# The first norm of a hybrid decoder: squares summed by two other routes, and new prices in the planner

## The chip, the cores and the metric

The kernel runs on one core of a Trainium2 chip. A core has five engines that work side by side, each through its own list of instructions in order: TensorE (PE; its weight loads are shown as PEld), VectorE (DVE), ScalarE (ACT), GpSimd (POOL) and SyncE (SP), which issues the DMA transfers. They wait for each other by semaphores. The metric is the time of one execution on the device in microseconds (us), lower is better. All times here are of executions on the chip.

## What is computed

Two layers over 1024 tokens of width 1024, in float32: a gated DeltaNet layer, then a layer with stick-breaking attention, each with a SwiGLU feed-forward and a gated per-layer embedding. The change concerns the first norm of the first layer:

```python
def rms_norm(x, g):
    xf = x.astype(jnp.float32)
    y = xf * lax.rsqrt(jnp.mean(xf * xf, axis=-1, keepdims=True) + EPS)
    return (y * g.astype(jnp.float32)).astype(x.dtype)

h = x
for i in range(DEPTH):
    hn = rms_norm(h, ln_mix[i])
    ...  # mixer, feed-forward, per-layer embedding
```

## The kernel before

Activations lie with features on the 128 partitions and tokens along the row: x is eight tiles (k = 0 to 7) of 128 features by 1024 tokens, and is worked on in two halves of 512 tokens (hf = 0, 1). Matrix products run on TensorE with float32 split in two parts, hi and lo, each rounded to float32r: a product is three passes (hi by hi, hi by lo, lo by hi), each with 512 columns. A unit is 128 output features of one half: 8 k times 3 passes, 24 products. Weights come by DMA into `raw` (two buffers); ScalarE casts them to `whi`, and VectorE or GpSimd subtracts to get `wlo`.

**What sets the order.** The program is written as Python generators: small tasks (a norm, the features of one head, a copy of a result) that issue a few instructions and yield. The class `Flow` steps through them at build time and keeps a clock for each engine with a price for each instruction (`cost`), a delay from one engine to the next (`lat`, `LAT`) and the time of transfers (`issued`). The task that is ready and has the best priority issues next, and where none is ready the stream of large products (`fill`) goes on. The engines' lists are thus fixed before the run. A price that changes can reorder instructions anywhere behind it; no instruction becomes longer or shorter by it.

**The start.** `gdn_start` holds four tasks. `load` issues the sixteen loads of x (`xT`, 256 KB each) on SP, in tiles named kt, Z, vt, QK, zz and ou. `norm(hf)` squares each of the eight tiles of a half on ScalarE (`sumsq`; scratch tiles Gb, four buffers), and VectorE adds the squares up in `LT`. Then `rstd` lets TensorE sum over the partitions: the sum tile is the stationary operand, a column of ones the moving one, so there are four products with one column each, one per 128 tokens, into a tile `tp`. `root` makes `ms` on VectorE and raises it to the power -1/2 on GpSimd (`rs`). `normed` broadcasts `rs` over the partitions with four products into another `tp`, and for each k VectorE multiplies x by it and the gain (`qf<-..,vec,tp`), ScalarE casts the result to float32r (`x<-qf`), and VectorE subtracts for the lo part (`x<-qf,x`).

Meanwhile `warm` issues products `mm<-triR` with 256 columns, whose results nobody reads, until the planner holds the first normed tile to be ready. Then `gdn_first` issues the first units of both halves, k by k as the tiles come: `ab` (tile `po`), k and q of head 0 (tiles `mm`, two buffers). For each unit `gdn_features` then empties `mm` on ScalarE (`xe<-mm`) and runs a short convolution over it (`ca`). `loads` issues the weights; it starts once all loads of the first half of x are issued.

**Behind the start** come the units of the first heads. `gdn_inv` prepares the decay matrices: broadcast loads `Gb<-gD`, a selection on GpSimd and 16 exponentials on ScalarE (`Gb<-Gb,nG`). `ple_products` makes the products of the second layer's embedding (tiles `rc`, `r`, `po`, `mm`); ScalarE copies each result to `sg` or `ca`, two buffers each, from which SP writes it to DRAM (`ppD`).

In the profile nearly every instruction has line 64, the helper through which all are issued, so tiles tell them apart.

Of the kernel before, what the change touches and what calls it, by code (L numbers as in the profile page):

```python
# [10 lines left out]
AF = mybir.ActivationFunctionType  # L11
ALU = mybir.AluOpType
# [3 lines left out]
P = 128  # L16
S = 1024
D = 1024
NK = D // P
H = 8  # L20
HW = 512
# [61 lines left out]
class Flow:  # L83
# [30 lines left out]
    def cost(self, eng, op, out, ins, kw):  # L114
        n = 1
        for d in (ins[0] if op == "tensor_reduce" else out).shape[1:]:
            n *= d
        psum = any(x.space == PSUM for x in ins)
        if eng == "pe":
            if op != "transpose" and ins[0].dtype == F32R:  # L120
                return max(n, P) / 2400.0 + 0.0127
            return max(n, P) * (2 if op == "transpose" else 4) / 2400.0 + (0.003 if op == "transpose" else 0.0107)
        if eng == "dve":
            if op == "memset":
                return 0.06 + n / 3840.0
            tail = 0.06 if any(x.shape[-1] == 1 for x in ins) and n > 1 else 0.0
            if any(x.shape[-1] > 1 and x.ap[-1][0] > 1 for x in ins):
                tail += 0.085
            fast = op in ("tensor_copy", "tensor_scalar") and not psum
            return 0.069 + tail + n / (1920.0 if fast else 960.0)  # L130
        if eng == "act":
            us = (0.052 if psum else 0.094) + n / 1200.0
            return us + 0.093 * (len(ins) - 1) + (0.235 if "accum_out" in kw else 0.0)
        if op == "tensor_tensor":
            return 0.295 + 0.166 * n if kw.get("op") == ALU.pow else 0.148 + n * 0.002104
        return 0.4 + n / 1400.0 if op == "affine_select" else 0.1 + n / 1085.0

    def shared(self, eng, op, outs, ins, kw, t, c):

# [22 lines left out]
    def issued(self, eng, op, args, kw):  # L162
        aps = [x for x in list(args) + list(kw.values()) if hasattr(x, "space")]
        if not aps:
            if op == "preload_act_table_set":
                self.table = 3
            return
        outs = [kw["out"] if "out" in kw else aps[0]]
        if "accum_out" in kw:
            outs.append(kw["accum_out"])  # L170
        ins = [x for x in aps if not any(x is o for o in outs)]
        t = self.clock[eng]
        if eng == "pe":
            t = max(t, self.now)
        spans = []
        for x, w in [(o, True) for o in outs] + [(i, False) for i in ins]:
            if x.space == DRAM:
                lo, dims = x.offset, x.ap
            else:
                dims, step = x.ap[1:], x.ap[0][0]  # L180
                lo = x.offset % step if step else x.offset
            hi = lo + 1 + sum((c - 1) * d for d, c in dims)
            rec = self.mem.get(x.name)
            if rec is None:
                rec = self.mem[x.name] = {}
                old = self.old.pop(x.name, None)
                if old is not None and old in self.mem:
                    t = max([t] + [max(v[0] + self.lat(v[1], eng), v[2] + self.lat(v[3], eng)) for v in self.mem.pop(old).values()])
            for (l, h), v in rec.items():
                if l < hi and lo < h:  # L190
                    if not (w and eng == v[1]):
                        t = max(t, v[0] + self.lat(v[1], eng))
                    if (w or x.space == PSUM) and v[3] != eng:
                        t = max(t, v[2] + self.lat(v[3], eng))
            spans.append((rec, (lo, hi), w))
        if eng == "dma":
            n = 4
            for d in outs[0].shape:
                n *= d
            run = min(x.ap[-1][1] if x.ap[-1][0] == 1 else 1 for x in outs + ins)  # L200
            n *= max(1, P // run)
            self.clock["dma"] = t + 0.475
            self.rings = max(self.rings, t + 1.1) + n / 360e3
            end = self.rings
        else:
            c = self.cost(eng, op, outs[0], ins, kw)
            f = [x for x in args if isinstance(x, AF)]
            if f and f[0] in TABLES and TABLES[f[0]] != self.table:
                self.table = TABLES[f[0]]
                t += 1.4  # L210
            if eng in ("dve", "pool"):
                t = self.shared(eng, op, outs, ins, kw, t, c)
            end = t + c
            self.clock[eng] = end
            if eng == "pe":
                self.now = end
        for rec, key, w in spans:
            v = rec.setdefault(key, [-1e9, eng, -1e9, eng])
            if w:
                v[0], v[1] = end, eng  # L220
            elif end > v[2]:
                v[2], v[3] = end, eng
        self.ready = max(self.ready, end + self.LAT[eng])

    def lat(self, a, b):
        if b == "pe":
            return {"pe": 0.0, "dma": 1.2}.get(a, 0.25)
        return 0.13 if a == b and a != "dma" else self.LAT[a]

    def run(self, fill):  # L230
        test = None
# [40 lines left out]
class Net:  # L272
# [155 lines left out]
    def weights(self):  # L428

        flow, nc = self.flow, self.nc  # L430
        reqs = self.weight_list()
# [10 lines left out]
                return "e"  # L442

        def loads():
            yield lambda: ("x", 0, NK - 1) in flow.at
            for key, src, _, _ in reqs:
                yield lambda: count["load"] - count["split"] < 2
                raw = self.t(self.wp, "raw", (P, NK, P), bufs=2)
                nc.sync.dma_start(raw, src)
                raws.append((raw, flow.ready))  # L450
                count["load"] += 1
                yield 0.5
# [39 lines left out]
        def splits():  # L492
            for i, (key, src, gain, cls) in enumerate(reqs):
# [12 lines left out]
                flow.spawn(done(), 3)  # L506

        flow.spawn(loads(), 4)
        flow.spawn(splits(), 3)

# [30 lines left out]
    def root(self, pool, st, r):  # L541
        nc = self.nc
        ms = self.t(pool, "ms", (P, 4))
        nc.vector.tensor_scalar(ms, st[:, :4], 1.0 / D, EPS, op0=ALU.mult, op1=ALU.add)
        self.unbank(st)
        yield
        nc.gpsimd.tensor_tensor(r, ms, self.nhalf[:, :4], op=ALU.pow)
        yield
# [136 lines left out]
    def gdn_start(self):  # L685

        nc, io, flow = self.nc, self.io, self.flow
        tags = ["kt"] * 4 + ["Z"] * 3 + ["vt"] * 3 + ["QK"] * 2 + ["zz"] * 2 + ["ou"] * 2
        src = {(hf, k): self.g(tags[hf * NK + k]) for hf in range(2) for k in range(NK)}

        def load():
            for hf in range(2):
                for k in range(NK):
                    nc.sync.dma_start(src[hf, k], io["xT"][k, :, hf * HW : (hf + 1) * HW])
                    flow.mark(("x", hf, k))
                    yield 0.4
            nc.sync.dma_start(self.ad, io["ad"])
            nc.sync.dma_start(self.conv, io["conv"])
            nc.sync.dma_start(self.masks, io["cst"][:, C_OFF:])
            nc.vector.memset(self.X0, 0.0)  # L700

        def norm(hf):
            acc = self.g("LT", (P, 2, HW))[:, 0]
            for k in range(NK):
                yield lambda: flow.done(("x", hf, k))
                yield from self.sumsq(lambda: self.g("Gb"), acc, src[hf, k], k == 0)
            r = self.g("rs", (P, 4))
            yield from self.rstd(self.gs, acc, r)
            yield from self.normed(("n0", hf), r, lambda k: src[hf, k], self.vec[:, 0], lambda: self.g("qf"))

        def ple():
            yield lambda: flow.done(("norm", ("n0", 1)))
            self.ple1 = [[self.g(tag, dt=F32R) for tag in tags] for tags in (("Z", "Z", "Z", "QK"), ("ou", "ou", "zz", "zz"))]
            flow.mark("ple1")
            yield from self.ple_operands(1, *self.ple1, "kt")

        flow.spawn(load(), 0)
        flow.spawn(norm(0), 0)
        flow.spawn(norm(1), 1)
        flow.spawn(ple(), 4)  # L720

# [1347 lines left out]
def layout(inputs):  # L2069

    g = {k: np.asarray(v) for k, v in inputs.items()}
# [12 lines left out]

    a = {}
    a["cst"] = const_table()
    a["xT"] = np.ascontiguousarray(g["x"][0].T).reshape(NK, P, S)
    a["pT"] = np.ascontiguousarray(g["p"][:, 0].transpose(0, 2, 1)).reshape(2, 2, P, S)
    vs = []
# [40 lines left out]
```

## Time and profile before

| | us |
|---|---|
| median of 3 runs | 2787.19 |
| lowest, highest run | 2784.03, 2788.08 |
| the profiled execution | 2787.44 |
| its span, first to last instruction | 2785.7 |

A row of the timeline has start and duration in us, the engine, the operation, output<-inputs by the program's names, shapes and a count of merged instructions; in brackets stands how long the engine had been idle before it, and for whom it waited. A row of a group has the count, the busy time in us and the mean of one in ns, then the idle time before them. A row of a window has its length, then busy time and number of instructions for each engine, TensorE's granted clock as a share of full speed, the busy share of the DMA engines and GB/s. TensorE's products overlap, and their ends are modelled: how far apart they start tells more than how long each one lasts. A product of plain float32 is recorded as two instructions.

### The profile page before, as it was taken

To read this page: it belongs to the slowest core of one execution; us is meant where nothing else is said; L and a number is where in the kernel's file an instruction comes from. 1 tells how busy PE (TensorE), PEld (TensorE's weight loads), DVE (VectorE), ACT (ScalarE), POOL (GpSimd) and SP (SyncE) were. 2 spreads that over 40 slices of the span, in tenths; PEclk is the share of its full clock that TensorE was granted. 3 is DMA by queue.
4 is the path that set the end of the run, shared out by engine and by line. 5 is a ranking of instruction groups with operands and counts; after the bars stand their busy time and mean duration, and the time that the engine had idled before them with its cause. 6 is when DMAs were issued, how large, how long until landed. Compare 5 with 4: busy or idle time off the path is not lost.

```text
span 2785.7 us, 37779 instructions
## 1 busy us (share of the span) xinstructions
PE 2741.7 (98%) x13203; PEld 2278.1 (82%) x13203; DVE 1951.7 (70%) x3733; ACT 1324.3 (48%) x2701; POOL 860.4 (31%) x742
## 2 busy tenths in 40 slices
PE   9999999999999999999999999999999999999999
PEld 8788888888778888888778888888878888888777
DVE  7687887873875665477857778887686565557783
ACT  6655555543433344322335778877443343322241
POOL 0111111100166667444101222221036666643400
PEclk9999999999999999999999999999999999999999
DMA  4412222247334444587232111114514444487623
GB/s 147 143 58 76 75 82 74 74 151 244 140 110 159 155 155 144 223 328 304 106 131 99 54 50 61 54 58 158 200 57 156 150 148 151 144 311 284 262 90 105
DMA packets 165072, 394.85 MB, mean 142 GB/s; under 512 B 34000, under 2 KB 35344, under 8 KB 155408
## 3 DMA queue, kind: packets, MB, share of 16 engines
q1 hardware_dynamic: 164880, 392.43, 39.5%
q8 instruction: 104, 1.70, 0.2%
q14 instruction: 88, 0.72, 0.1%
HBM read 273.77 MB, written 118.59 MB: 141 GB/s over the span
## 4 chain that ended last, share of the span: by engine, by line
PE 86%; DVE 7%; ACT 4%; issue 2%; DMA 1%; POOL 1%; ACTq 0%; POOLq 0%
PE dn L64 38%; PE mm L64 34%; PE tp L64 4%; PE z L64 3%; PE c L64 2%; PE o L64 2%; DVE x L64 1%; PE po L64 1%; PE rc L64 1%; PE r L64 1%; DVE u L64 1%; ACT junk L64 1%; ACT L64 1%; DVE v L64 1%; PE st L64 1%
## 5 line engine op out<-in xcount | busy, mean ns | idle before, releaser
L64 PE MATMUL mm<-x,whi 128*128 128x512 f32 x2848 | 939.0, 400 | 8.7 <-DVE x L64 5.4
L64 PEld LDWEIGHTS mm<-x,whi 128*128 128x128 f32 x2848 | 528.5, 189 | 106.7 <-DVE x L64 7.9
L64 PE MATMUL mm<-x,wlo 128*128 128x512 f32 x1424 | 568.5, 399 | 0.0
L64 PE MATMUL dn<-x,whi 128*128 128x512 f32 x1776 | 548.7, 390 | 1.8 <-DVE x L64 0.9
L64 POOL TENSOR_TENSOR wlo<-raw,whi 128x512 fp32r<-128x512 f32 x236 | 345.5, 1485 | 442.7 <-ACT whi L64 413.2
L64 ACT CAST whi<-raw 128x1024 fp32r<-128x1024 f32 x231 | 242.8, 1051 | 447.4 <-DVE raw L64 244.7
L64 PEld LDWEIGHTS dn<-x,whi 128*128 128x128 f32 x1776 | 333.3, 188 | 73.3 <-DVE x L64 2.6
L64 PE MATMUL dn<-x,wlo 128*128 128x512 f32 x888 | 345.7, 389 | 0.0
L64 PEld LDWEIGHTS mm<-x,wlo 128*128 128x128 f32 x1424 | 269.0, 189 | 46.4 <-issue 0.3
L64 PE MATMUL dn<-hx,whi 128*128 128x512 f32 x864 | 267.4, 390 | 0.4 <-DVE hx L64 0.2
L64 DVE TENSOR_TENSOR tt<-u,tt 128x512 fp32r<-128x512 f32 x140 | 143.9, 1028 | 81.5 <-ACT tt L64 81.5
L64 PEld LDWEIGHTS dn<-x,wlo 128*128 128x128 f32 x888 | 166.7, 188 | 34.4
L64 PEld LDWEIGHTS dn<-hx,whi 128*128 128x128 f32 x864 | 162.8, 189 | 35.0 <-DVE hx L64 0.6
L64 DVE TENSOR_TENSOR v<-v,dn 128x512 f32<-128x512 f32 x112 | 76.5, 684 | 155.4 <-PE dn L64 155.0
L64 DVE TENSOR_TENSOR wlo<-raw,whi 128x512 fp32r<-128x512 f32 x226 | 153.9, 693 | 27.2 <-ACT whi L64 26.9
L64 PE MATMUL dn<-hx,wlo 128*128 128x512 f32 x432 | 169.1, 391 | 3.4 <-POOL wlo L64 3.4
L64 POOL TENSOR_TENSOR wlo<-sw,whi 128x512 fp32r<-128x512 f32 x102 | 144.3, 1431 | 2.0 <-ACT whi L64 2.0
L64 ACT CAST tt<-u 128x512 fp32r<-128x512 f32 x140 | 84.8, 619 | 123.5 <-DMA yD<-tt 100.2
L64 DVE TENSOR_TENSOR E<-E,dn 128x512 f32<-128x512 f32 x132 | 90.0, 684 | 71.4 <-PE dn L64 69.1
L64 POOL TENSOR_TENSOR rs<-ms,nhalf 128x4 f32<-128x4 f32 x11 | 12.3, 1122 | 330.7 <-DVE ms L64 330.7
L64 PE MATMUL dn<-y,whi 128*128 128x512 f32 x352 | 108.4, 389 | 0.0
L64 DVE SCALAR_TENSOR_TENSOR ca<-xe,conv,ca 128x512 f32<-128x512 f32 x144 | 106.2, 744 | 0.9 <-ACT ca L64 0.4
(376 smaller groups left out, 5124.8 us busy)
## 6 DMA issues: line engine op xcount, KB each, us to landing
yD<-tt SPq DMA_DIRECT2D x296, 256.0 KB, 2.4
x<-yD SPq DMA_DIRECT2D x58, 1024.0 KB, 11.3
raw<-f_s SPq DMA_DIRECT2D x84, 512.0 KB, 3.7
raw<-d_s SPq DMA_DIRECT2D x40, 512.0 KB, 5.9
raw<-w_in SPq DMA_DIRECT2D x33, 512.0 KB, 4.0
hx<-yD SPq DMA_DIRECT2D x16, 1024.0 KB, 14.5
x<-oD SPq DMA_DIRECT2D x26, 512.0 KB, 5.8
raw<-g_out SPq DMA_DIRECT2D x16, 512.0 KB, 5.2
```

Source lines behind the costliest of these rows:

```text
L64: r = issue(*args, **kw)
```

## The change

It has two parts.

**The first norm.** For the first half TensorE sums the squares itself: each of the eight square tiles is the stationary operand of four one-column products that accumulate in one `tp` tile, with no adds on VectorE. For the second half a copy of x with tokens on the partitions, `xr` (4 blocks of 128 tokens by 1024 features, 512 KB each, made on the host from the same input), is loaded into `LT` tiles, and ScalarE squares each with `accum_out`, which leaves the sums in `ms` without TensorE. The four loads of `xr` come ahead of the second half of `xT`; `LT` has two buffers, so the third and fourth wait for squares of the first two. The first two weights are issued ahead of `xr` (the mark `first`); that weights start after the eighth x tile is as before (`NK` is 8). The zeroing of `X0` moves from VectorE to GpSimd, to the very start.

**The prices.** Short float32r products have a floor of 0.1 us; a subtraction on GpSimd costs a little more and a selection less; a load that spreads one row over all partitions lands 1.4 us later; and two instructions of VectorE in a row need 0.06 us between them in place of 0.13.

```diff
@@ cost, issued, lat
-                return max(n, P) / 2400.0 + 0.0127
+                return max(n / 2400.0 + 0.0127, 0.1)
...
-            return 0.295 + 0.166 * n if kw.get("op") == ALU.pow else 0.148 + n * 0.002104
-        return 0.4 + n / 1400.0 if op == "affine_select" else 0.1 + n / 1085.0
+            return 0.295 + 0.166 * n if kw.get("op") == ALU.pow else 0.169 + n * 0.002125
+        return 0.119 + n / 960.0 if op == "affine_select" else 0.1 + n / 1085.0
...
+            spread = any(x.ap[0][0] == 0 for x in ins)
-            self.rings = max(self.rings, t + 1.1) + n / 360e3
+            self.rings = max(self.rings, t + (2.5 if spread else 1.1)) + n / 360e3
...
-        return 0.13 if a == b and a != "dma" else self.LAT[a]
+        return {"dve": 0.06, "dma": self.LAT["dma"]}.get(a, 0.13) if a == b else self.LAT[a]
@@ loads (weights)
-            yield lambda: ("x", 0, NK - 1) in flow.at
-            for key, src, _, _ in reqs:
+            yield lambda: ("x", 0, 7) in flow.at
+            for n, (key, src, _, _) in enumerate(reqs):
+                if n == 2:
+                    flow.mark("first")
@@ gdn_start: load
+        rows = {}
             for hf in range(2):
+                if hf == 1:
+                    yield lambda: "first" in flow.at
+                    for j in range(4):
+                        rows[j] = self.g("LT", (P, 2, HW))
+                        nc.sync.dma_start(rows[j].rearrange("p a c -> p (a c)"), io["xr"][j])
+                        flow.mark(("xr", j))
+                        if j == 1:
+                            yield lambda: flow.done("sq1")
+                        else:
+                            yield 0.4
...
-            nc.vector.memset(self.X0, 0.0)
@@ gdn_start: norm
-            acc = self.g("LT", (P, 2, HW))[:, 0]
-            for k in range(NK):
+            r = self.g("rs", (P, 4))
+            if hf == 0:
+                st = yield from self.bank()
+            else:
+                ms = self.t(self.gs, "ms", (P, 4))
+                for j in range(4):
+                    yield lambda: flow.done(("xr", j))
+                    nc.scalar.activation(rows[j], rows[j], AF.Square, accum_out=ms[:, j : j + 1])
+                    if j == 1:
+                        flow.mark("sq1")
+                yield
+                yield from self.root(self.gs, ms, r)
+            for k in range(NK * (1 - hf)):
                 yield lambda: flow.done(("x", hf, k))
-                yield from self.sumsq(lambda: self.g("Gb"), acc, src[hf, k], k == 0)
-            r = self.g("rs", (P, 4))
-            yield from self.rstd(self.gs, acc, r)
+                sq = self.g("Gb")
+                nc.scalar.activation(sq, src[hf, k], AF.Square)
+                yield
+                for j in range(4):
+                    self.mmul(st[:, j : j + 1], sq[:, j * P : (j + 1) * P], self.ones[:, :1], k + j == 0, k == NK - 1, True)
+            if hf == 0:
+                yield
+                yield from self.root(self.gs, st, r)
...
+        nc.gpsimd.memset(self.X0, 0.0)
@@ layout (host)
+    a["xr"] = np.ascontiguousarray(g["x"].reshape(S, D)[HW:].reshape(4, P, D))
```

How the lists move is shown at three places. The first is TensorE's list from its start (`x4`, `x73` and the like count equal instructions in a row; `ones` is a part of `cst`). Before:

```order
L64 MATMUL mm_126<-triR 128x256 x73
L64 MATMUL tp_32_252<-cst,LT_128 128x1 x4
L64 MATMUL mm_126<-triR 128x256 x16
L64 MATMUL tp_38_286<-cst,rs_251 128x128 x4
L64 MATMUL mm_126<-triR 128x256 x36
L64 MATMUL po_351<-x_291,whi_246 128x512 x2
```

There the fillers in front, between and behind the sum and the broadcast are 125. TensorE's list from its start, after the change:

```order
L64 MATMUL mm_127<-triR 128x256 x22
L64 MATMUL tp_19_131<-cst,Gb_154 128x1 x4
L64 MATMUL tp_19_131<-cst,Gb_167 128x1 x4
L64 MATMUL tp_19_131<-cst,Gb_174 128x1 x4
L64 MATMUL tp_19_131<-cst,Gb_180 128x1 x4
L64 MATMUL tp_19_131<-cst,Gb_186 128x1 x4
L64 MATMUL tp_19_131<-cst,Gb_192 128x1 x4
L64 MATMUL tp_19_131<-cst,Gb_198 128x1 x4
L64 MATMUL tp_19_131<-cst,Gb_204 128x1 x4
L64 MATMUL mm_127<-triR 128x256 x14
L64 MATMUL tp_40_247<-cst,rs_130 128x128 x4
L64 MATMUL mm_127<-triR 128x256 x21
```

The fillers are 57 now, and eight groups of one-column products stand in a row with none between them.

The second place is SP's list behind the first eight loads of x. After the change (before, the loads of `xT` go on to ou there, with two loads of `raw` between them):

```order
L64 DMA raw_210<-w_in 128x1024
L64 DMA raw_225<-w_in 128x1024
L64 DMA LT_236<-xr 128x1024
L64 DMA raw_238<-w_in 128x1024
L64 DMA LT_245<-xr 128x1024
L64 DMA raw_257<-w_in 128x1024
L64 DMA LT_313<-xr 128x1024
L64 DMA LT_319<-xr 128x1024
L64 DMA vt_118<-xT 128x512
```

Four weights and the four blocks of `xr` now stand ahead of the second half of `xT`, of which vt_118 is the first.

The third place is ScalarE's list around the first exponentials of `Gb`. Before (688, 777, 829 and 883 are units that follow the first q on TensorE, in this order):

```order
L64 COPY xe_774<-mm_688 128x512
L64 ACT_TABLE_LOAD
L64 ACTIVATE EE<-vt_690 128x192
L64 ACT_TABLE_LOAD
L64 ACTIVATE beta<-vt_635 128x64
L64 COPY xe_824<-mm_777 128x512
L64 CAST whi_826<-raw_714 128x1024
L64 ACTIVATE ca_833<-xe_774,conv 128x512
L64 ACTIVATE ca_837<-xe_824,conv 128x512
L64 ACT_TABLE_LOAD
L64 ACTIVATE Gb_724<-Gb_724,nG 128x128 x4
```

The units 688 and 777 are copied out of `mm` ahead of the exponentials. ScalarE's list at the same place after the change, where the units behind the first q are 636, 713, 791 and 830:

```order
L64 COPY xe_710<-mm_636 128x512
L64 ACTIVATE EE<-vt_619 128x192
L64 ACT_TABLE_LOAD
L64 ACTIVATE beta<-vt_579 128x64
L64 ACT_TABLE_LOAD
L64 ACTIVATE qf_747<-ca_683 128x512
L64 ACTIVATE ca_753<-xe_710,conv 128x512
L64 ACT_TABLE_LOAD
L64 ACTIVATE Gb_650<-Gb_650,nG 128x128 x4
L64 ACTIVATE Gb_651<-Gb_651,nG 128x128 x4
L64 ACTIVATE Gb_658<-Gb_658,nG 128x128 x4
L64 ACTIVATE Gb_659<-Gb_659,nG 128x128 x4
```

The copy of unit 713 is no longer ahead of the exponentials: it is the next instruction behind these rows, and unit 830 uses the same buffer of `mm` as 713.

More of the change, by code (lines that the diff above doesn't have):

```diff
@@ L544, in root @@
         nc.vector.tensor_scalar(ms, st[:, :4], 1.0 / D, EPS, op0=ALU.mult, op1=ALU.add)
-        self.unbank(st)
+        if st.name in self.held:
+            self.unbank(st)
         yield
```

## The prediction

> **What bounds the kernel now.** The page's head comes first, to see which engine sets the end: busy time, share of the span and instructions of each.
>
> ```profile
> span 2785.7 us, 37779 instructions
> PE 2741.7 (98%) x13203; PEld 2278.1 (82%) x13203; DVE 1951.7 (70%) x3733; ACT 1324.3 (48%) x2701; POOL 860.4 (31%) x742
> ```
>
> TensorE is idle for 2785.7 - 2741.7 = 44.0 us in all. So a change to the first norm can win only what TensorE does not spend on real products: idle time, fillers, and time at a low clock. The timeline of the start, rows of several engines in order, shows the fillers (`mm<-triR`, results thrown away).
>
> ```profile
> 4.20 11.50 PE L64 MATMUL mm<-triR 128*128 128x256 f32 x73 [4.20 <-DVE triR L64]
> 7.64 0.63 ACT L64 ACTIVATE LT<-kt 128x512 f32<-128x512 f32 x1 [5.56 <-DMA kt<-xT]
> 15.54 0.95 PE L64 MATMUL tp<-cst,LT 128*128 128x1 f32 x8
> 16.77 1.38 POOL L64 TENSOR_TENSOR rs<-ms,nhalf 128x4 f32<-128x4 f32 x1 [16.26 <-DVE ms L64]
> 18.34 1.05 PE L64 MATMUL tp<-cst,rs 128*128 128x128 f32 x8
> 19.15 4.56 PE L64 MATMUL mm<-triR 128*128 128x256 f32 x36
> 21.96 0.68 DVE L64 TENSOR_TENSOR x<-qf,x 128x512 fp32r<-128x512 f32 x1
> 23.55 0.62 PE L64 MATMUL po<-x,whi 128*128 128x512 f32 x2
> 43.27 0.62 PE L64 MATMUL po<-x,whi 128*128 128x512 f32 x2
> ```
>
> Sums of squares are ready for the root at 16.49, the first real product starts at 23.55, and the products of the second half start at 43.27. The product at 23.55 is held by the 36 fillers: its operand was complete at 22.64. From there on it is busy throughout, as this window behind it shows (length, then the busy time of TensorE, its weight loads, VectorE, ScalarE, POOL):
>
> ```profile
> 54.35:79.99 25.64, 25.64 (x124) 20.75 (x123) 16.59 (x38) 25.22 (x47) 4.26 (x6) 1.00 0.32 106
> ```
>
> So 43.27 is the mark against which I measure the start.
>
> **The squares on TensorE.** The change drops the seven adds on VectorE for each half (14 in all) and gives TensorE eight groups of four products with one column each, recorded as eight instructions.
>
> ```profile
> L64 DVE TENSOR_TENSOR LT<-LT,Gb 128x512 f32<-128x512 f32 x14 | 9.5, 681 | 5.3 <-ACT Gb L64 4.8
> 4.00:9.00 5.00, 4.80 (x22) 4.80 (x23) 0.22 (x2) 1.34 (x3) 0.00 (x0) 1.00 0.87 279
> 9.00:14.00 5.00, 5.00 (x41) 5.00 (x40) 4.31 (x7) 4.18 (x7) 0.00 (x0) 1.00 1.04 405
> ```
>
> An add took 0.68 us against 0.63 us for its square, so the adds kept pace with ScalarE and only the last one stood on the path. A group of one-column products took 0.95 us (row of 15.54). Fillers cost 4.80/22 = 0.218 us each in the first window and 5.00/41 = 0.122 us in the second: TensorE starts at half its rate, although the clock column reads 1.00 there. Now 22 fillers come first: 4.20 + 22 x 0.218 = 9.0. Eight groups at 0.95 us end at 16.6, against 16.49 before. **Even at full clock the squares are ready no earlier.**
>
> But will the clock be full? Here are windows further on; behind the busy times stands the granted clock.
>
> ```profile
> 2692.00:2696.00 4.00, 2.58 (x16) 1.78 (x14) 4.00 (x7) 0.96 (x2) 0.00 (x0) 1.00 0.47 154
> 2696.00:2699.00 3.00, 3.00 (x11) 2.40 (x10) 2.28 (x5) 0.89 (x2) 1.01 (x1) 0.53 0.37 147
> 2040.00:2044.00 4.00, 4.00 (x15) 3.52 (x14) 0.51 (x1) 0.00 (x0) 3.53 (x3) 0.50 0.39 131
> 98.00:104.00 6.00, 2.48 (x13) 1.77 (x11) 3.27 (x9) 2.22 (x10) 1.01 (x1) 1.00 0.68 214
> 2037.05 1.51 PE L64 MATMUL st<-cst,acc 128*128 128x1 f32 x8 [0.28 <-DVE acc L64]
> 2038.41 0.77 PE L64 MATMUL mm<-hx,whi 128*128 128x512 f32 x1
> ```
>
> After a stretch with idle time and one group of one-column products (2692 to 2696) the clock was halved, and it stayed halved through 2040 to 2044 although TensorE was busy. One-column products therefore seem to count as little work. At half clock such a group takes 2038.41 - 2037.05 = 1.36 us. Eight of them in a row are a far longer such stretch, so I expect the half clock: 9.0 + 8 x 1.36 = 19.9, or about 18.3 if the first groups still run at full clock.
>
> [...]
>
> **To the first product.** VectorE's ms, then POOL's root (1.38), need about 1.7 us, and 14 fillers lie over that: 1.7 us at 0.122, 3.0 at half clock (0.218). The broadcast of the root is 1.05 us (1.5 in the ratio 1.36 to 0.95), then 21 fillers 2.6 us. Full clock: 16.6 + 1.7 + 1.05 + 2.6 = 21.95. Half, until the fillers have released it: 19.9 + 3.0 + 1.05 + 2.5 = 26.4 (24.4 from the other start). Before: 23.55.
>
> The first half is then 72 products, paced by these:
>
> ```profile
> 23.16 0.74 DVE L64 SCALAR_TENSOR_TENSOR qf<-kt,vec,tp 128x512 f32<-128x512 f32 x1
> 23.82 0.68 DVE L64 TENSOR_TENSOR x<-qf,x 128x512 fp32r<-128x512 f32 x1
> 54.15 0.61 PE L64 MATMUL mm<-x,whi 128*128 128x512 f32 x2
> L64 ACT CAST x<-qf 128x512 fp32r<-128x512 f32 x13 | 8.0, 619 | 12.8 <-DVE qf L64 12.8
> L64 ACT ACTIVATION_READ_ACCUMULATOR junk<-tp 128x1 f32 x8 | 1.6, 196 | 0.0
> ```
>
> The 48 products from 43.27 to 54.15 took 0.227 us each, so 72 take 16.3, and the second broadcast 1.05. For six products (1.36 us) VectorE makes one multiply (0.66 to the next start) and one subtraction (0.68 at most): without the adds, and with the zeroing of X gone to POOL (where nothing waits for it: POOL idles until 16.77), it just keeps up, save for two splits of weights. ScalarE's squares of 1024 columns with a sum have no row: they lie between twice a square's 0.63 and that plus a read of the accumulator, 0.2; I take 1.3, as it is nearer the second. Four make 5.2 us, and eight casts 5.0, which hides under 17 us. If rows of x came late, the casts queued behind the square on ScalarE would wait, and through them VectorE and the products. I count 1.5 us of such waits at full clock and 0.5 at half, where all else is earlier than needed. Marks: 21.95 + 17.4 + 1.5 = 40.8 (**-2.5**), or 26.4 + 17.4 + 0.5 = 44.3 (+1.0), or 42.3 to 43.0 from 24.4 (-0.6). I take **+0.4** for the half clock, between the two and nearer the first: the 22 fillers alone end before or about when the fast window of 9 to 14 begins. SP now sends x's second half last, behind a square (LT has two buffers) and behind splits; some 2.9 MB at the 400 GB/s of the window are in by 36 to 38, before use. If that cover went, each us late would cost a us.
>
> **ScalarE after the start.** These are groups of ScalarE between 54.3 and 80 (busy, mean ns, idle), and the rows at the ends.
>
> ```profile
> L64 ACT ACT_TABLE_LOAD x8 | 10.3, 1283 | 0.1
> L64 ACT CAST whi<-raw 128x1024 fp32r<-128x1024 f32 x4 | 4.2, 1041 | 0.0
> L64 ACT ACTIVATE ca<-xe,conv 128x512 f32<-128x512 f32 x4 | 2.8, 717 | 0.0
> L64 ACT COPY xe<-mm 128x512 f32<-128x512 f32 x4 | 2.3, 576 | 1.0 <-PE mm L64 1.0
> 54.35 0.59 ACT L64 COPY xe<-mm 128x512 f32<-128x512 f32 x1 [0.98 <-PE mm L64]
> 79.99 4.79 ACT L64 ACTIVATE Gb<-Gb,nG 128x128 f32<-128x128 f32 x16
> 85.99 0.40 PE L64 MATMUL rc<-Z,whi 128*128 128x512 f32 x1
> ```
>
> ScalarE has no slack here: the 16 exponentials start 25.64 us after the copy at 54.35. Now one table load, one cast, one copy and one ca fewer stand ahead of them (1.28 + 1.04 + 0.58 + 0.72 = 3.6 us busy, 3.4 as each starts a little before the last has ended), so they start 22.25 us after it and end 4.8 later. But the copy that empties `mm` for the last unit of v (24 products) now stands **behind** them: 22.25 + 4.8 + 0.5 and 0.4 for signals = 27.9 us after the end of the first units. TensorE gets there after 85.99 - 54.15 = 31.84, less that unit's 5.44 and 0.81 for eight transpositions (18.34 to 19.15 is such a group): 25.6. So it waits **2.3 us** where it did not wait before. Bounds: 0 if ScalarE gains on the rows, 4 if the clock halves in the gap.
>
> **The first products of the embedding**, with their waits:
>
> ```profile
> 92.36 1.16 PE L64 MATMUL tp<-qf,kf 128*128 128x128 f32 x8 [0.47 <-ACT vt L64]
> 103.72 0.50 PE L64 MATMUL r<-Z,whi 128*128 128x512 f32 x1 [3.52 <-ACT sg L64]
> 112.24 0.50 PE L64 MATMUL mm<-Z,whi 128*128 128x512 f32 x1 [1.78 <-ACT ca L64]
> 103.08 0.59 ACT L64 COPY sg<-r 128x512 f32<-128x512 f32 x1 [3.08 <-DMA ppD<-sg]
> 98.70 0.39 SPq L64 DMA_DIRECT2D ppD<-sg  x1
> ```
>
> The 3.52 us are a chain: SP holds the write of sg until 98.70 behind a second load of eGb, so ScalarE gets its buffer back at 103.08. After the change the copies alternate between ca and sg, but the first write stands behind the same load, and a copy that waits for it stands ahead of a kf that TensorE needs: about 4.3 us there against 3.52 + 1.78 + 0.47 = 5.77. I take **-1.5**, bounds -5.8 and +2.
>
> **The rest.** The planner's prices also reorder the delta rule and the attention; the feed-forward keeps TensorE's order. Such waits are small already:
>
> ```profile
> 1934.27 0.50 PE L64 MATMUL o<-wh,vh 128*128 128x512 f32 x1 [1.05 <-DVE wh L64]
> 1935.00:1942.00 7.00, 6.62 (x20) 5.63 (x21) 4.24 (x12) 4.96 (x9) 1.32 (x3) 0.51 0.08 29
> ```
>
> Here a wait of 1.05 us, with a few short ones beside it, was followed by 7 us at a clock of 0.51 (3.4 us lost). The new order has products around it but asks for `wh` sooner. I put 0 for the rest, bounds -6 and +6.
>
> **Sum**, against the profiled execution of 2787.44 (span and 1.74 around it; the median of the runs is 0.25 below it): 2787.44 + 0.4 + 2.3 - 1.5 = 2788.6, or **2788.4** as a median.
>
> **Rivals.** A measurement can tell about 0.2% from no change, 5.6 us: 2781.6 to 2792.8.
> - Full clock in the squares (22%): -2.5 in place of +0.4, 2785.5. For it: 98 to 104 kept its clock over a gap of 3.5 us. Against it: the halved rows above.
> - The two waits on ScalarE halve the clock (18%), slower: 2.3 us at the `mm` copy and 4.3 at kf, each followed by half clock as at 2696 (3 us, 1.5 lost) or at 1935 (7 us, 3.4 lost), 4.9 in all: 2793.3. It decides where idle time and light work fill about half of a few us, as at 2692, where 4.00 - 2.58 = 1.42 us of idle and one light group of 0.95 sufficed in 4. Against it stands the gap of 3.5 us at 100.
> - The new prices take away the wait at the end of the attention and its half clock (1.05 + 3.4), and the squares run at full clock (12%): 2788.4 - 4.45 - 2.9 = 2781.0.
> - My forecast has the remaining 48%.
>
> **Range and chances.** 2781 to 2796: it reaches the fast rival and holds the slow one with the bound of the rest. Faster 0.13 (the last rival and the edge of the first), same 0.68, slower 0.19 (the slow rival and the forecast's upper edge).
>
> **What would show it.** Right: one-column groups at 1.3 us or more in the squares, or a granted clock near 0.5 up to about 23; the first real product after 24; second-half products at 42 to 45; a wait of TensorE on a copy to xe of 1.5 to 3.5 us near 79; a wait near 100 on ScalarE. Wrong: groups at 0.95 us and the mark at 41, no wait near 79, or waits of more than 5 us in all in the delta rule or attention that were not there.

## The result

The changed kernel took 2810.06 us (median of 4 runs, 2807.87 to 2813.0) against 2787.64 before (4 runs): a ratio of 1.0084, 95% interval 1.0066 to 1.0101. It is 22.4 us slower (25.3 between the two profiled spans), beyond the range of the prediction. The head of the profile's page after:

```profile
span 2811.0 us, 37778 instructions
PE 2752.8 (98%) x13183; PEld 2276.7 (81%) x13183; DVE 1941.2 (69%) x3718; ACT 1321.1 (47%) x2700; POOL 863.6 (31%) x743
```

TensorE is idle for 58.2 us where it was 44.0, and busy for 11.1 us more with 20 instructions fewer. Four points of TensorE's timeline that both kernels have divide the loss: the first product of the second half, the first sum on `st` (the norm behind the delta rule), the last product of the first feed-forward and the first of the second.

| stretch | before | after | |
|---|---|---|---|
| start to the second half's first product | 43.3 | 45.0 | +1.7 |
| to the first sum on `st` (units, delta rule) | 671.7 | 690.4 | **+18.7** |
| to the last product of feed-forward 1 | 666.8 | 669.6 | +2.8 |
| to the first product of feed-forward 2 (attention) | 669.7 | 674.6 | +4.9 |
| to the end of the span | 734.2 | 731.4 | -2.8 |

So the question is the second stretch. First the start, which the prediction worked out. TensorE's timeline after, then windows (length, busy time of TensorE, its loads, VectorE, ScalarE, POOL, granted clock):

```profile
8.40 11.50 PE L64 MATMUL tp<-cst,Gb 128*128 128x1 f32 x64
27.05 0.62 PE L64 MATMUL po<-x,whi 128*128 128x512 f32 x2
44.98 0.62 PE L64 MATMUL po<-x,whi 128*128 128x512 f32 x2
```

```profile
8.00:12.00 4.00, 4.00 (x33) 4.00 (x31) 0.00 (x0) 3.75 (x7) 0.00 (x0) 0.85 1.04 389
12.00:24.00 12.00, 12.00 (x58) 12.00 (x58) 2.65 (x5) 4.06 (x6) 1.38 (x1) 0.50 0.40 139
```

The eight groups take 11.50 us, 1.44 each on the mean; from 12 us on the clock is 0.50 although TensorE does not pause. The mean mixes two rates. Here are the first two groups, then two of the later ones:

```profile
8.40:10.13 1.73, 1.73 (x18) 1.73 (x17) 0.00 (x0) 1.68 (x3) 0.00 (x0) 1.00 1.00 361
12.93:16.35 3.42, 3.42 (x18) 3.42 (x18) 0.69 (x1) 2.92 (x4) 0.00 (x0) 0.50 0.44 180
```

A group takes 0.87 us at full clock and 1.71 at half clock.

Now the second stretch as one window, of before and then of after:

```profile
43.27:715.00 671.73, 661.45 (x3710) 558.07 (x3708) 494.60 (x1396) 370.27 (x989) 61.61 (x78) 1.00 0.34 113
```

```profile
44.98:735.40 690.42, 670.14 (x3710) 558.11 (x3708) 496.75 (x1393) 368.47 (x987) 59.39 (x78) 1.00 0.34 110
```

The same 3710 products, and the other engines as busy as before: no work was added. Idle time grew from 10.3 to 20.3 us, and 8.7 us are TensorE "busy" with the same products. Of these the half clock behind one long wait makes 2.6 (0.50 x 4 + 0.15 x 4 in the last two windows; in the first of the three, at 0.80, TensorE mostly waits). The wait, then the windows:

```profile
108.19 1.12 PE L64 MATMUL tp<-cst,kf 128*128 128x128 f32 x4 [3.81 <-ACT kf L64]
104.00:108.00 4.00, 0.38 (x2) 0.00 (x0) 3.07 (x10) 1.56 (x3) 1.02 (x1) 0.80 0.74 282
108.00:112.00 4.00, 3.81 (x11) 3.23 (x12) 3.66 (x14) 3.15 (x12) 0.08 (x1) 0.50 0.32 119
112.00:116.00 4.00, 4.00 (x19) 3.27 (x18) 3.50 (x12) 1.57 (x3) 1.67 (x2) 0.85 0.44 167
```

Part of the rest hides in weight loads that wait. In the view of one tile, the engines' idle time before instructions that touch it is listed by what ended it. For `vin`, the input that VectorE makes for each step of the recurrence, before and after (us, times; the second row of each is the part of TensorE's weight loads):

```profile
  DVE vin L64: 6.0, 21
  PEld r L64: 5.3, 19
```

```profile
  DVE vin L64: 11.9, 32
  PEld r L64: 9.5, 27
```

VectorE is no busier, but delivers late. The growth, 5.9 us, is under a third of the 18.7; TensorE's other waits in this stretch are spread over kf, vf, vn, kt, xr and ou, 1.5 to 3.8 us each, and nothing here ties each of them to one price. The timelines of VectorE and of TensorE show one such place after the change (rows between left out):

```profile
445.48 0.26 DVE L64 TENSOR_TENSOR yr<-xr,Ls 128x96 f32<-128x96 f32 x1
...
448.94 0.30 DVE L64 TENSOR_REDUCE xr<-yr 128x8 f32<-128x144 f32 x1
449.28 0.31 DVE L64 TENSOR_TENSOR yr<-xr,Ls 128x144 f32<-128x144 f32 x1
449.51 0.35 DVE L64 SCALAR_TENSOR_TENSOR vin<-rc,neG,vt 128x128 f32<-128x128 f32 x1
```

```profile
447.19 0.39 PE L64 MATMUL rc<-Sm,kf 128*128 128x128 f32 x2
449.91 0.49 PE L64 MATMUL r<-vin,Z 128*128 128x128 f32 x2 [0.90 <-DVE vin L64]
```

`rc`, which `vin` needs, was done at 447.58. But `vin` stands in VectorE's list behind the steps of a block inversion (`yr`, `xr`: each needs the one before), and starts 1.9 us later. From `yr` 128x96 to `yr` 128x144 are twelve steps, 3.80 us. The planner's price of a step is 0.069 + n/960 and the delay between two instructions of VectorE, which the planner adds only where the second reads what the first wrote. Summed over these twelve it gives 3.89 with a delay of 0.13 and **3.05 with 0.06**. So over these twelve steps the new plan holds VectorE to be free 0.75 us sooner than it is, and TensorE waited 0.90. The steps take as long in the trace of before, where VectorE's timeline has

```profile
112.62 0.30 DVE L64 TENSOR_TENSOR yr<-xr,Ls 128x136 f32<-128x136 f32 x1
112.96 0.30 DVE L64 TENSOR_REDUCE xr<-yr 128x8 f32<-128x144 f32 x1
332.50 0.74 DVE L64 SCALAR_TENSOR_TENSOR ca<-xe,conv,ca 128x512 f32<-128x512 f32 x1
333.28 0.75 DVE L64 SCALAR_TENSOR_TENSOR ca<-xe,conv,ca 128x512 f32<-128x512 f32 x1
```

A step of 136 elements starts its successor 0.34 us later; the old price says 0.34, the new one 0.27. The two `ca`, of which the second reads the first, start 0.78 apart; the price, with the planner's 0.06 for the operand of one column, is 0.79 with 0.13 and 0.72 with 0.06. Where the next instruction does not depend on the last (449.28 to 449.51), it starts 0.23 later, which is the 0.069 + n/960 of 144 elements (0.22) with next to no delay.

### The profile page after: what moved, and what is told of

It is laid out like the page before. It is cut to its first block, busy times and chain, and to the rows that moved or that the text cites. A ratio compares the mean times of both kernels' runs of the same rounds, so it can differ in the third digit from the quotient of the medians.

```text
span 2811.0 us, 37778 instructions
## 1 busy us (share of the span) xinstructions
PE 2752.8 (98%) x13183; PEld 2276.7 (81%) x13183; DVE 1941.2 (69%) x3718; ACT 1321.1 (47%) x2700; POOL 863.6 (31%) x743
## 4 chain that ended last, share of the span: by engine, by line
PE 72%; DVE 6%; issue 2%; DMA 2%; ACT 1%; POOL 1%; SPq 0%; POOLq 0%; ACTq 0%; DVEq 0%
PE dn L64 36%; PE mm L64 26%; PE z L64 3%; PE c L64 2%; PE o L64 2%; PE tp L64 1%; DVE x L64 1%; DMA raw<-d_s 1%; DVE u L64 1%; DVE v L64 1%; PE st L64 1%; DVE hx L64 1%; DVE wlo L64 0%; POOL wlo L64 0%; DVE y L64 0%
## 5 line engine op out<-in xcount | busy, mean ns | idle before, releaser
L64 DVE TENSOR_TENSOR tt<-u,tt 128x512 fp32r<-128x512 f32 x140 | 137.0, 979 | 82.5 <-ACT tt L64 82.3
L64 POOL TENSOR_TENSOR rs<-ms,nhalf 128x4 f32<-128x4 f32 x11 | 11.9, 1078 | 331.3 <-DVE ms L64 331.1
```

The costliest lines, as they stand in the source:

```text
L64: r = issue(*args, **kw)
```

## The experiments

The theory (P) is that the prices, and among them the 0.06, cause the loss; its rivals are the new norm (N) and that any new order costs (A, later R). "st" below is the start of the first sum on `st`: 715.0 before, 735.4 after. In the first four expectations the point called the first transposition of X is wrongly named: 601.8 and 618.6 are the starts of the last group but one of such transpositions. That point came at 607.0 us in e1, 616.3 in e2, 609.3 in e3 and 621.5 in e4; the readings below go by st.

**The change in two parts.**

```diff
# e1: the diff of the norm (loads, root, gdn_start, host), prices of before
# e2: the diff of cost, issued, lat; norm of before
```

> The new first norm with the old prices. Reference points are the start of the first transposition of X (601.8 us before, 618.6 after) and the last product of the kernel. Theory N (the norm does it: the squares at half clock and the new order that follows from later first products) expects 2805 to 2812 us and the point at 615 to 619. Theory P (the new prices do it) expects 2786 to 2792 us and the point at 601 to 605: only the later start of the first products remains. Theory A (any new order of the delta rule costs, whatever caused it) expects 2795 to 2808 us and the point at 608 to 618. All three: half clock in the squares and the first real product near 27 us, and the attention as before.

> The new prices with the old first norm. Theory N expects 2784 to 2792 us and the first transposition of X at 601 to 604 us. Theory P expects 2803 to 2812 us and that point at 614 to 619. Theory A expects 2795 to 2808 us and 608 to 617. All three: the start as before (first real product near 23.5 us), and the attention of the changed kernel, whose end costs the 4 to 5 us more that lay between 1388 and 1960 us.

The norm alone: 2787.87 us, ratio 1.0009 (1.0 to 1.0019), st 717.4. The prices alone: 2811.03, ratio 1.0091 (1.0076 to 1.0106), st 733.7. Theory N falls. Theory A falls in its plain form: the norm moves several hundred of the first 2600 products in TensorE's list and yet takes only 1.3 us more from its second-half mark to st (717.4 - 44.4 = 673.0 against 671.7).

**Single prices on the kernel before.**

```diff
# e3
+            spread = any(x.ap[0][0] == 0 for x in ins)
-            self.rings = max(self.rings, t + 1.1) + n / 360e3
+            self.rings = max(self.rings, t + (2.5 if spread else 1.1)) + n / 360e3
# e4
-        return 0.13 if a == b and a != "dma" else self.LAT[a]
+        return {"dve": 0.06, "dma": self.LAT["dma"]}.get(a, 0.13) if a == b else self.LAT[a]
# e8
-                return max(n, P) / 2400.0 + 0.0127
+                return max(n / 2400.0 + 0.0127, 0.1)
```

> The kernel before with one price alone: a broadcast read lands 2.5 us after its issue in the plan instead of 1.1. The delta rule gets another order, the attention none. Theory A expects the first transposition of X at 606 us or later (601.8 before) and 5 us or more in all; theory P, if this price is the one at fault, 614 to 619; theory N, and P if another price is at fault, 600 to 604 and 2784 to 2792 us.

> The kernel before with one price alone: the time between two instructions of VectorE is 0.06 us in the plan instead of 0.13. The delta rule and the attention get other orders. Theory A expects the first transposition of X at 606 us or later; theory P, if this price is the one at fault, 614 to 619; theory N, and P if another price is at fault, 600 to 604.

> The kernel before with one price alone: a product of TensorE costs 0.1 us at least in the plan. TensorE's order changes in the attention alone. If this price is what made the stretch from the end of the first feed-forward (1381.8 us before) to the second's first product (2051.5) 4 to 5 us longer with all prices (1402.3 to 2076.1 and 1405.0 to 2079.6 against 669.7 before), that stretch is 673 to 675 us; if another price did it, 669 to 671. In all 2784 to 2793 us.

Each of these three is one run. e3: st 722.0, 2791.0 us. e4: st **736.4**, 2810.3 us: one number in one line gives the whole loss. e8: st 716.0, 2784.9 us, and the stretch from feed-forward to feed-forward is 666.1 us, less than either case had: the floor is not what lengthens the attention. The price of e3 is nearer to the trace than the old one, and still costs 7 us at st, as theory A had it (609.3 at its point, 5 us in all). The old plan lands such a load 1.8 us after its issue (1.1, and 0.73 for 256 KB at 360 KB/us), the new one 3.2; the groups of DMA issues of before (count, KB each, median us from issue to landing) say

```profile
Gb<-gD SPq DMA_DIRECT2D x16, 256.0 KB, 4.3
eGb<-gD SPq DMA_DIRECT2D x16, 256.0 KB, 3.6
```

**The changed kernel without the 0.06.**

```diff
-        return {"dve": 0.06, "dma": self.LAT["dma"]}.get(a, 0.13) if a == b else self.LAT[a]
+        return 0.13 if a == b and a != "dma" else self.LAT[a]
```

> The changed kernel with one price put back: 0.13 us between two instructions of VectorE instead of 0.06. Reference point: the start of the first sum on st behind the delta rule (715.0 us before, 735.4 after, 736.4 with the 0.06 alone, 722.0 with the landing of broadcast reads alone, 717.4 with the new norm alone). Theory L (the 0.06 is what costs) expects the point at 717 to 725 us and 2788 to 2798 us in all. Theory S (prices that don't fit each other: whatever is put back, the delta rule stays near 20 us late) expects 730 to 738 and 2804 to 2813.

2797.54 us, ratio 1.0037 (1.0025 to 1.005); st 720.4 with the whole of the rest of the change, 15 us earlier than after. Its view of `vin`:

```profile
  DVE vin L64: 4.9, 19
  PEld r L64: 4.6, 18
```

Theory S falls. 11.7 us of the medians remain; of the 9.0 between the profiled spans, 5.4 are there at st, and 3.2 come in feed-forward 1.

**Which steps of VectorE.**

```diff
+        self.chain = outs[0].name.split("_")[0] in ("yr", "xr")
...
+        if a == b == "dve":
+            return 0.06 if self.chain else 0.13   # e7; e6: 0.13 if self.chain else 0.06
```

> The kernel before with 0.06 us between instructions of VectorE, except for those that write xr and yr (the 62 dependent steps of each block inversion), which keep 0.13. Theory C (the plan believes the inversions are 4.3 us shorter each than they are, and that is what costs) expects the first sum on st at 714 to 719 us. Theory V (every pair of VectorE is priced too short, the recurrence's own among them, and those cost) expects 728 to 738.

> The kernel before with 0.06 us between the dependent steps of the inversions (those that write xr and yr) alone, 0.13 for the rest. Theory C expects the first sum on st at 728 to 738 us. Theory V expects 714 to 719. If both parts cost, 718 to 728 here and in the run with the inversions at 0.13.

e7 (inversions alone too short): st 734.4, 2802.1 us. e6 (all others too short): st 725.5, 2800.5. Both cost, the inversions more: 19.4 and 10.5 us, and they don't add (e4 has 21.4). So theory C holds for e7 and misses e6, and theory V misses both. The wait on `vin` belongs to the inversions; e7's view of it, and its window from 43.27 us to st with the 3710 products:

```profile
  DVE vin L64: 14.7, 32
  PEld r L64: 11.3, 27
```

```profile
43.27:734.40 691.13, 672.12 (x3710) 561.32 (x3709) 496.66 (x1396) 369.85 (x989) 59.40 (x78) 0.99 0.34 110
```

In e6 the wait on `vin` is 3.9 us.

**Is it the misfit, or any new order?** The same edit with other numbers for the inversions' steps, 0.13 for the rest, and one price that touches no step of VectorE.

```diff
# e9, e10, e11, e13, e14
+            return V if self.chain else 0.13      # V = 0.10, 0.16, 0.20, 0.12, 0.14
# e15, on the kernel before
-        return 0.4 + n / 1400.0 if op == "affine_select" else 0.1 + n / 1085.0
+        return 0.119 + n / 960.0 if op == "affine_select" else 0.1 + n / 1085.0
```

> The kernel before with 0.10 us between the dependent steps of the inversions, 0.13 for the rest. The trace has 0.34 us from yr 128x136 to the step behind it, where the plan has 0.34 with 0.13 and 0.27 with 0.06. Theory C (the loss follows from how far the plan's step is too short) expects the first sum on st at 718 to 727 us, between 715.0 with 0.13 and 734.4 with 0.06, and the waits of VectorE's and TensorE's other work on vin in between. Theory R (any new order of the delta rule costs a few us up to some twenty, by chance) expects no order among 0.06, 0.10, 0.16 and 0.20: somewhere from 715 to 736 here.

> The same with 0.16 us, a plan whose steps are 0.03 us too long. Theory C expects the first sum on st at 713 to 719 us (a plan that asks too late idles nothing it can fill with other products), theory R anywhere from 715 to 736, and so as often above 722 as below.

> The same with 0.20 us, 0.07 too long, as far off as 0.06 but to the other side. Theory C expects the first sum on st at 713 to 722 us, theory R 715 to 736; a theory that any error of the step costs, whatever its sign, expects 728 to 738 as with 0.06.

> The kernel before with 0.12 us between the dependent steps of the inversions, 0.01 from the old price and within what the trace can tell from it. Theory F (a plan holds as long as its step fits the chip's 0.34 us; beyond some hundredths it costs 10 us or more) expects the first sum on st at 713 to 722 us. Theory R (orders scatter by 10 us and more, and the old one was a good draw) expects it anywhere from 715 to 736, so above 722 as likely as not.

> The same with 0.14 us: theory F 713 to 722 us, theory R anywhere from 715 to 736.

> The kernel before with the new price of affine_select alone; VectorE's steps keep 0.13. The delta rule gets another order (the same number of rows of TensorE stand elsewhere as with all new prices), and the attention too. Theory F expects the first sum on st at 713 to 722 us, theory R anywhere from 715 to 736.

| delay in the inversions | st | us, one run | idle on `vin` |
|---|---|---|---|
| 0.06 (e7) | 734.4 | 2802.1 | 14.7 |
| 0.10 (e9) | 727.9 | 2800.1 | 4.5 |
| 0.12 (e13) | 718.0 | 2789.2 | 4.7 |
| 0.13 (before) | 715.0 | 2785.7 to 2787.6, medians | 6.0 |
| 0.14 (e14) | 714.5 | 2783.0 | 4.8 |
| 0.16 (e10) | 727.0 | 2796.9 | 4.0 |
| 0.20 (e11) | 726.1 | 2798.6 | 2.9 |
| 0.13, select price (e15) | 723.2 | 2797.8 | 3.2 |

It looks like a valley: within 0.01 of the old price the order moves too (several hundred of the first 2600 products) and costs 3 us at most; from 0.03 on either side it costs 11 us and more. Theory C is half right: 0.06 is the worst, but steps priced too long cost as well, which it did not expect. It also misses e9, where it expected longer waits on `vin`: they are 4.5 us, less than before, and st is 12.9 us later all the same. So late `vin` goes with the 0.06 alone, and there its waits grow by 8.7 us where st comes 19.4 later (e7). In e11 the waits on `vin` are the smallest; its loss is in single long waits and the half clock behind them, as in this row and these windows of it:

```profile
210.75 1.25 PE L64 MATMUL tp<-cst,ou 128*128 128x128 f32 x4 [3.72 <-ACT ou L64]
```

```profile
208.00:212.00 4.00, 1.25 (x5) 1.02 (x6) 0.92 (x5) 2.17 (x10) 1.01 (x1) 0.54 0.41 131
212.00:216.00 4.00, 4.00 (x16) 3.50 (x16) 2.91 (x11) 0.62 (x1) 0.00 (x0) 0.60 0.39 142
```

e15 misses theory F's bound by a us: an order can lose 7 to 8 us (e3, e15) with steps that fit. So scatter is real, and theory R is not ruled out for the 11 to 13 us of 0.10, 0.16 and 0.20: each was seen once, and how a step priced too long leads to such waits was not tried. What stands out of the scatter is the 0.06 in the inversions. From the second half's first product to st, the four kernels that have it (after, e2, e4, e7) take 18.7 to 21.7 us longer than the kernel before; the thirteen others take from 0.1 less to 13.3 more. (The four share that price, so they are not four independent orders.)

**The norm's two halves.**

```diff
 def norm(hf):
     if hf == 0:
+        acc = self.g("LT", (P, 2, HW))[:, 0]
+        for k in range(NK):
+            yield lambda: flow.done(("x", hf, k))
+            yield from self.sumsq(lambda: self.g("Gb"), acc, src[hf, k], k == 0)
...
-        self.mmul(st[:, j : j + 1], sq[:, j * P : (j + 1) * P], self.ones[:, :1], k + j == 0, k == NK - 1, True)
```

> The kernel with the new norm alone and the old prices, in which the squares of the first half are summed on VectorE again as before the change; the second half's stay on ScalarE. TensorE's order is that of the new norm alone but for 13 rows at the start. If the squares on TensorE at half clock are what that kernel lost, the first real product starts at 23.3 to 24.3 us (27.2 with them, 24.2 before), the first sum on st at 713.5 to 715.5 (717.4 with them) and the time is 2784 to 2786.5 us. If the new order of the delta rule lost it, the first product is early all the same and the sum on st still at 716.5 to 718.5, 2786.5 to 2789 us in all.

> The squares of the second half on ScalarE, those of the first on VectorE as before, the old prices, and the floor of 0.1 us for TensorE's products: the delta rule in the order that reached st at 712.4 us in 2783.6 us in all, the attention in that of the floor alone (666.1 us from the end of the first feed-forward to the first product of the second, against 669.7). If the two gains add, 2779 to 2782 us against 2786 to 2787 before, and 666 to 667 us for that stretch; if the attention's gain in one look was a chance of the clock, 2783 to 2785.

e12: 2783.56 us, ratio 0.9986 (0.9977 to 0.9995), so 0.14% below the kernel before by an interval that just leaves out 1, and 26 us below the changed one; st 712.4 and the first product at 21.84, both earlier than was expected. Its timeline and a window:

```profile
14.55 1.05 PE L64 MATMUL tp<-cst,LT 128*128 128x1 f32 x8
21.84 0.50 PE L64 MATMUL po<-x,whi 128*128 128x512 f32 x1
```

```profile
9.00:14.00 5.00, 5.00 (x44) 5.00 (x43) 4.35 (x7) 4.19 (x7) 0.00 (x0) 1.00 1.04 408
```

Its second half starts at 39.9 us, 3.4 before the old one and 4.6 before e1, from whose order it differs only at the start. So the rest of the new norm gains 3.4 us (1.7 of them are there at the first product, 21.84 for 23.55), and the squares on TensorE lose 4.6. e16, with the floor of e8 on top: 2781.64, ratio 0.9985 (0.9976 to 0.9994). Its stretch between the feed-forwards is 666.8 us against 669.6 in e12, but the two medians can't be told apart.

## Why the prediction was wrong

- **The step that failed** is "I put 0 for the rest, bounds -6 and +6". It looked at how long TensorE waited before, found little to win, and gave the order of the delta rule no sign. What the runs show in its place: of the 25.3 us between the spans, the terms of the sum make 5.1 (1.7, 1.0 and 2.4, below) and the rest makes 20.2. The stretch to st alone grew by 18.7 us; the 0.06 alone makes st 21.4 later (e4), and without it st is 15 earlier (e5). The price's truth was not weighed against the rows of VectorE, though they were in the trace: 0.34 us from one step of 136 elements to the next. The inversions alone have 496 steps (248 `yr`, as many `xr`), 0.07 us short each, up to 35 us of VectorE's time that the new plan doesn't count. Of the signs named, "waits of more than 5 us in all in the delta rule" came true.
- **The squares**: sums at 19.8 for 19.9, first product at 27.05 for 26.4, mark at 44.98 for 44.3. That the clock would be half came true, and the rival of a full clock fell; that the sums came to 19.8 is partly luck. The price of 1.36 us was read from a group of before that ran at half clock in part only, as its own window shows:

```profile
2037.05:2038.41 1.36, 1.36 (x8) 1.36 (x9) 0.45 (x1) 1.07 (x2) 1.16 (x1) 0.63 0.00 0
```

  At 0.50 a group takes 1.71, but the first two groups still ran at full clock, 0.87 each, and the errors cancel. (The half clock of 2040 to 2044 stands behind this group, not behind the stretch at 2692.) The broadcast of the root, which the sum had at 1.05, took 1.56 at half clock (22.89 to 24.45). The +0.4 taken instead of the full +1.0 was too small: it was +1.7 (the same instructions at the start put the mark at 44.4 in e1 and 44.8 in e5). It rested on a first product at 24.4, for which the prediction's own terms (18.3 + 3.0 + 1.05 + 2.5) give 24.8. The clock of 0.50 came under products that follow each other without a gap: TensorE was busy for 12.00 us of the 12.00 from 12 to 24.
- **ScalarE late at `xe`**: the copy does stand behind the exponentials, but TensorE waited 0.96 us, not 2.3. The mechanism was right and the size off, below the 1.5 us that were named as a sign.

```profile
83.56 0.50 PE L64 MATMUL mm<-x,whi 128*128 128x512 f32 x1 [0.96 <-ACT xe L64]
```

- **The embedding** (-1.5): the waits before kf and kt are 3.81 + 1.79 = 5.6 for 5.77, a gain of 0.2, and the half clock behind the first adds 2.6: +2.4 in all. That is half of the second rival; behind the wait at `xe` the clock was 1.00 (83.56 to 92.00).
- **The attention's end** went against the third rival. TensorE's waits and a window there:

```profile
1960.35 0.50 PE L64 MATMUL o<-wh,vh 128*128 128x512 f32 x1 [1.75 <-DVE wh L64]
1964.05 0.79 PE L64 MATMUL mm<-x,whi 128*128 128x512 f32 x1 [1.93 <-ACT x L64]
```

```profile
1963.00:1970.00 7.00, 5.95 (x18) 4.99 (x19) 3.85 (x10) 3.66 (x9) 0.88 (x3) 0.52 0.10 37
```

  The waits are 3.7 us for 1.05, and the half clock stays. Which price does it is open: the floor alone shortens that stretch (666.1), the 0.06 alone leaves it (670.1), the price of the selection alone makes 673.2 (e15), but all prices without the 0.06 make 670.3 (e5), and all together 673.7 (e2) and 674.6.
- **Feed-forward 1** was taken as unchanged. TensorE's order is, but after, e1, e5 and e12 take 669.6 to 670.2 us there, the other runs 665.0 to 668.7. e16 has that norm too and takes 666.3; what makes the 3 us stays open.

## What to carry to other kernels

A price in a planner is a statement on the chip, so hold it against start-to-start times of dependent rows before it goes in: here two rows would have told. A change of prices that adds and removes no work can still cost more than all other edits. One way is seen here: an engine that is planned as free too early delays what stands behind it in its list (idle on `vin` 11.9 us for 6.0); it explains a part of the loss, not all. Even a price that comes nearer to the trace has to be run by itself, as the broadcast loads show.

## What the runs showed of the hardware

- Under one-column products issued without a pause TensorE's clock did not stay whole: it was 1.00 from 8.40 to 10.13 us after and 0.50 from 12.00 to 19.85, and came back only behind the fillers and the broadcast that follow (0.50 to 24.45, 1.00 from 24.45 to 27.05). Where fillers of 256 columns stand from 9 to 14 us (e12) it is 1.00, at 5.00/44 = 0.114 us each.
- The length of a wait alone did not tell the clock behind it: behind a wait of 3.52 us in the kernel before it was 1.00 (103.72 to 107.72), behind one of 3.81 after it was 0.50 (108 to 112), and so it was behind one of 1.89 in e11:

```profile
606.52 0.59 PE L64 MATMUL tp<-cst,ou 128*128 128x128 f32 x2 [1.89 <-ACT ou L64]
607.71:611.12 3.41, 3.41 (x10) 2.67 (x9) 3.41 (x8) 0.62 (x1) 0.00 (x0) 0.50 0.32 80
```

- On VectorE an instruction that needs the result of the last started about 0.11 us later than one that doesn't: after the change 0.34 us behind a step of 144 elements (448.94 to 449.28) against 0.23 (449.28 to 449.51). The recorded durations don't show it: these two steps are recorded with 0.30 and 0.31 us. In the kernel before, a step of 136 elements is recorded with 0.30 us, and its dependent successor starts 0.34 us behind it (112.62 to 112.96).
